# Attention's scores of layer 0 in the attention's own pair of PSUM banks

## The chip, the cores and the metric

One Trainium2 chip; the program runs on one of its cores. The metric is device time in microseconds of one execution, as the median of three runs.

## What is computed

The reference is a trunk of two layers over 256 tokens of width 2048, in float32. Each layer normalises and modulates its input, projects it, runs three mixers side by side (gated linear attention, a gated delta rule, differential attention), gates and concatenates their outputs and projects them back. Cut to what matters:

```python
for l in range(DEPTH):                                   # DEPTH = 2
    shift, scale, gate = split(c_act @ w_ada[l] + b_ada[l], 3)
    h = rms_norm(x, norm_w[l]) * (1 + scale) + shift
    (gq, gk, gv, glr, gz, dq, dk, dv, da, db, dz, aq, ak, av, az) = split(h @ w_in[l], bounds)
    o_gla = rms_norm(gla_chunked(...)) * silu(gz)        # width 512
    o_gdn = rms_norm(gated_delta_chunked(...)) * silu(dz)  # width 512
    # differential attention: 4 heads, two score maps each, D = 128, values 256 wide
    s = einsum('bhmqd,bhmkd->bhmqk', q, k) * scale       # causal
    p = softmax(s)
    o_diff = rms_norm((p[:, :, 0] - lam * p[:, :, 1]) @ v) * (1 - lam_init) * silu(az)
    y = concatenate([o_gla, o_gdn, o_diff]) @ w_out[l]
    x = x + gate * y
```

## The kernel before

The 256 tokens are two tiles of 128 (t = 0, 1). Weights come from HBM in blocks of 128x1024 (`weights`): SP issues the transfer into a ring of six raw buffers, ACT casts them to the high part `wh` (L309), DVE subtracts to get the low part `wl` (L311), and TensorE forms three products per block (high by high, high by low, low by high). The in-projection writes its results into `pt` and `pf`, the out-projection into `py`, and DVE adds `py` to the residual stream (`xr`, L1262). The out-projection runs in three phases, by the rows of w_out: phase 0 takes the linear attention's output, phase 1 the delta rule's (`ogg`), phase 2 the attention's (`odf`). Beside all this the w_ada products of the next layer run in the gaps: SP loads a block into the same ring as `rawa` (L347), DVE multiplies and sums it (L327), and ACT finishes pairs of them (`ada_j`, L339).

PSUM has eight banks in three groups: four of p for the projections, two of a and two of b (`BANKS`, handed out by `bank`). Pair a belongs to the delta rule until that has been recorded; after that `free_a()` is true and gates take it too. Pair b serves the linear attention (`o_gla`), the rope transposes, and the attention's `aT_ps` and `o_diff`. A bank is given again only when its last reader is through.

The delta rule `gdn` ends with its state update `S_ps` on TensorE, `S_gdn` on DVE (L888), `wS_ps` on TensorE, `vn` on DVE (L876), `o_gdn` on TensorE and its copy `on_gdn` on ACT (L903). Then come squares on ACT (L563), a short chain on POOL (L907 to L912) and the gate product `z` on POOL (L1036). `gate_out` transposes z into `oT_ps`, and ACT (L1046) and DVE (L1047) split it into the operands of py, of phase 1 for the delta rule (`ogg`).

The attention (`diff_attend`) has eight tiles per layer, four heads by two query tiles, two in flight at a time. A tile runs: scores into `s_ps` (TensorE), causal mask (DVE L967, ACT L969), row maximum (DVE L971, L974), two exponentials (ACT L977), the combination coefficients (DVE L980, L982) and the difference (DVE L983), transposes `aT_ps` (TensorE) copied by ACT (L989), the product with the values `o_diff` (TensorE), its copy (ACT L995) and squares (ACT L563), five small steps on POOL for `r_o` (L999 to L1003), and the scaling (DVE L1004). The last gate takes the eight tiles' output in two halves (DVE L1036, `oT_ps`, L1046, L1047, `odf`) into phase 2.

Each step is a generator that yields between pieces. A task list with urgencies records the instructions, and a scheduler with its own estimate of times then puts them in a fixed order for each engine. Every engine executes its list strictly as it is written; the waits between engines are semaphores. So a different bank for a tile can change the order in which the scheduler lists everything around it. In layer 1 the in-projection's blocks are still running while its linear attention and delta rule are on: `L654` is the copy of `o_gla` to SBUF, `L452` a copy of projected features, `L671`, `L673` and `L674` the convolution and its silu on ACT and DVE, `QK_ps` and `Z_ps` the delta rule's products.

Of the kernel before, what the change touches and what calls it, by code (L numbers as in the profile page):

```python
# [144 lines left out]
def hybrid_trunk(ctx: ExitStack, tc: tile.TileContext, x, cvec, pos, par, w_ada, w_in, w_out, w_lr, qkn, adt, cst, out):  # L145
# [23 lines left out]
    def bank(name, tag):  # L169


        return psum.tile([P, 512], F32, name=name, tag=tag, bufs=BANKS[tag])

    def tiny(name, n, bufs=2):
        return small.tile([P, n], F32, name=name, tag=name, bufs=bufs)
# [6 lines left out]
    def mm(o, lhsT, rhs, start=True, stop=True, fast=False, **kw):  # L182
        clock[0] += rhs.shape[-1] * (0.00042 if fast else 0.0017)
        return PE.matmul(o, lhsT=lhsT, rhs=rhs, start=start, stop=stop, **kw)  # L184

    def transpose(o, i):
        clock[0] += 0.11
        PE.transpose(out=o, in_=i, identity=ident)
# [82 lines left out]
    def cc(name, n=128, off=0):  # L271
        return ct[:, CST[name] + off:CST[name] + off + n]
# [102 lines left out]
    def row_power(o, v, n):  # L375
        POOL.tensor_tensor(o, v, mhalf[:, 0:n], ALU.pow)
# [170 lines left out]
    def heads(ap, n=4):  # L547
        return ap.rearrange("p (h d) -> p h d", h=n)

    def over_heads(ap, n=4, d=128):  # L550
        return ap.rearrange("p (o d) -> p o d", o=1).broadcast_to([P, n, d])
# [6 lines left out]
    def head_norm(src, n, width, r):  # L558

        for h in range(n):  # L560
            a = junk_n[0] % (256 // width) * width
            junk_n[0] += 1
            ACT.activation(junk[:, a:a + width], src[:, width * h:width * h + width], AF.Square, accum_out=r[:, h:h + 1])  # L563
# [389 lines left out]
    def diff_attend(l, o, g, on, scr, free_a):  # L953
        causal = cc("causal")
        qT = lambda t, i: o.aqk[:, t, 0, 128 * i:128 * i + 128]
        kT = lambda t, i: o.aqk[:, t, 1, 128 * i:128 * i + 128]
        yield YW[22]

        def one_tile(h, t, turn):
            W = 128 * (t + 1)  # L960
            pb = bank("s_ps", "a" if free_a() else "b")
            for m in range(2):
                for k in range(t + 1):
                    mm(pb[:, W * m + 128 * k:W * m + 128 * k + 128], qT(t, 2 * h + m), kT(k, 2 * h + m))
            s = scr[:, (1 + turn) % 7]
            sv, pv = heads(s[:, 0:2 * W], 2), heads(pb[:, 0:2 * W], 2)
            DVE.tensor_tensor(sv[:, :, W - 128:W], pv[:, :, W - 128:W], over_heads(causal, 2), ALU.add)  # L967
            if t == 1:
                ACT.copy(sv[:, :, 0:128], pv[:, :, 0:128])  # L969
            mxs = tiny("mx_s", 2)  # L970
            DVE.tensor_reduce(mxs, sv, AX.X, ALU.max)  # L971
            sc = g.sq[t][:, 2 * h:2 * h + 2]
            nb = tiny("nb", 2)
            DVE.scalar_tensor_tensor(nb, mxs, -1.0, sc, ALU.mult, ALU.mult)  # L974
            sm = tiny("sm", 2)
            for m in range(2):
                ACT.activation(sv[:, m, :], sv[:, m, :], AF.Exp, bias=nb[:, m:m + 1], scale=sc[:, m:m + 1],  # L977
                               accum_out=sm[:, m:m + 1])
            rsm = tiny("rsm", 2, 4)
            DVE.reciprocal(rsm, sm)  # L980
            cf = tiny("cf", 1)
            DVE.scalar_tensor_tensor(cf, sm[:, 0:1], nlam[:, l:l + 1], rsm[:, 1:2], ALU.mult, ALU.mult)  # L982
            DVE.scalar_tensor_tensor(sv[:, 0, :], sv[:, 1, :], cf, sv[:, 0, :], ALU.mult, ALU.add)  # L983
            yield YW[23]
            pa = bank("aT_ps", "b")
            for k in range(t + 1):
                transpose(pa[:, HS[k]], sv[:, 0, HS[k]])
            aT = scr[:, 7, 256 * (turn % 2):256 * (turn % 2) + 256]
            ACT.copy(aT[:, 0:W], pa[:, 0:W])  # L989
            yield YW[24]  # L990
            po = bank("o_diff", "b")[:, 0:256]
            for k in range(t + 1):
                mm(po, aT[:, HS[k]], o.av[:, k, 256 * h:256 * h + 256], k == 0, k == t)
            d = o.aqk[:, t, 0, 256 * h:256 * h + 256]
            ACT.copy(d, po)  # L995
            r = tiny("r_o", 1, 4)
            head_norm(d, 1, 256, r)
            rs = rsm[:, 0:1]
            POOL.tensor_tensor(r, r, rs, ALU.mult)  # L999
            POOL.tensor_tensor(r, r, rs, ALU.mult)  # L1000
            POOL.tensor_scalar(r, r, 1.0 / 256.0, EPS, ALU.mult, ALU.add)
            row_power(r, r, 1)
            POOL.tensor_tensor(r, r, rs, ALU.mult)  # L1003
            DVE.tensor_scalar(d, d, r, None, ALU.mult)  # L1004
            yield YW[25]

        running = []
        todo = [(h, t) for h in range(4) for t in range(2)]
        turn = 0
        while todo or running:  # L1010
            if todo and len(running) < 2:
                h, t = todo.pop(0)
                running.append([clock[0], one_tile(h, t, turn)])
                turn += 1
            item = min(running, key=lambda r: r[0])
            if item[0] > clock[0]:
                yield item[0] - clock[0]
                continue
            w = next(item[1], None)
            if w is None:  # L1020
                running.remove(item)
            else:
                item[0] = clock[0] + w
        for t in range(2):
            on[t] = o.aqk[:, t, 0, :]
# [64 lines left out]
    with tc.issue_after(last_fold.ins), tc.issue_after(squared.ins), tc.issue_after(spread.ins):  # L1090
# [3 lines left out]
        pb = bank("lam_ps", "a")  # L1094
# [11 lines left out]
    for l in range(L):  # L1106
# [78 lines left out]
        def free_a():  # L1185
            return run["gdn"]["done"]
# [184 lines left out]
```

## Time and profile before

| | us |
|---|---|
| median of three runs | 1107.8 (1104.52 to 1108.89) |
| profiled execution | 1106.04 |
| its span | 1103.9 |
| TensorE busy in it | 1045.9 |
| DVE busy in it | 892.6 |
| ACT busy in it | 604.2 |
| POOL busy in it | 219.5 |

The span is the time between the first and the last instruction that the profiler saw, 2.1 us less than the device time of the same execution. Starts in the rows below count from the beginning of the span. A record of TensorE is often a part of one product of the program, since a float32 product is run in several passes; a py product is one record, a score product is two.

### The profile page before, as it was taken

The numbers are of one execution on the slowest core, as the hardware profiler recorded it, in microseconds if no ns is written. First come the engines' busy times: TensorE is split into PE (matmuls) and PEld (weight loads), VectorE is DVE, ScalarE is ACT, GpSimd is POOL, SyncE is SP. The second block draws the span as 40 slices with busy tenths as digits, with TensorE's granted clock in tenths as the row PEclk, the third lists the DMA queues.
The fourth block names the chain that finished last, engine by engine and source line by source line (L and its number), as shares of the span: only waits on it lengthen the run. The fifth ranks groups of instructions, "written<-read, shape, count | busy, mean of one in ns | idle before, by whom it ended". The sixth has DMA issues, their size and how long they took to land.

```text
span 1103.9 us, 19674 instructions
## 1 busy us (share of the span) xinstructions
PE 1045.9 (95%) x7398; PEld 915.2 (83%) x7398; DVE 892.6 (81%) x1373; ACT 604.2 (55%) x1244; POOL 219.5 (20%) x279
## 2 busy tenths in 40 slices
PE   5989999999899989969898999999999999999998
PEld 5769888888898868959796777899899877889998
DVE  7899999989999878759768687676856878687974
ACT  4845544447655726446545555458554556557642
POOL 0000000040210941133430000014232244202400
PEclk9999999999999989969998999999999999999999
DMA  9989999988977646744578898796544656677462
GB/s 366 348 280 343 340 332 337 317 312 320 317 253 249 192 148 225 269 144 142 165 247 293 319 341 307 262 301 229 180 125 159 212 181 198 223 244 238 134 210 96
DMA packets 76799, 273.24 MB, mean 248 GB/s; under 512 B 8816, under 2 KB 9888, under 8 KB 76576
## 3 DMA queue, kind: packets, MB, share of 16 engines
q1 hardware_dynamic: 76416, 271.80, 71.8%
q8 instruction: 58, 0.95, 0.3%
q14 instruction: 37, 0.30, 0.1%
q10 hardware_dynamic: 288, 0.19, 0.1%
HBM read 267.76 MB, written 4.19 MB: 246 GB/s over the span
## 4 chain that ended last, share of the span: by engine, by line
PE 61%; DVE 16%; DMA 10%; issue 7%; ACT 3%; POOL 2%; DVEq 0%; ACTq 0%; POOLq 0%; SPq 0%
PE pt L184 30%; PE py L184 14%; PE pf L184 8%; DMA rawa<-in_w_ada 7%; DVE wl L311 5%; DVE rawa L327 4%; DMA raw<-in_w_in 2%; ACT wh L309 1%; PE Z_ps L184 1%; PE s_ps L184 1%; PE o_diff L184 1%; PE Y_ps L184 1%; PE o_gla L184 1%; DVE fr L327 1%; DVE on_gdn L673 1%
## 5 line engine op out<-in xcount | busy, mean ns | idle before, releaser
L309 ACT CAST wh<-raw 128x1024 fp32r<-128x1024 f32 (+2 forms) x310 | 318.0, 1028 | 283.4 <-PE pt L184 131.5
L311 DVE TENSOR_TENSOR wl<-raw,wh 128x1024 fp32r<-128x1024 f32 (+2 forms) x310 | 382.1, 1238 | 60.6 <-ACT wh L309 57.6
L184 PE MATMUL pt<-wl,hh 128*128 128x512 f32 (+1 forms) x768 | 293.0, 384 | 4.6 <-DVE wl L311 4.5
L327 DVE SCALAR_TENSOR_TENSOR rawa<-rawa,c_row 128x1024 f32<-128x1024 f32 x184 | 228.3, 1245 | 80.5 <-DMA rawa<-in_w_ada 79.4
L184 PE MATMUL pt<-wh,hl 128*128 128x512 f32 (+1 forms) x768 | 288.8, 380 | 1.2 <-DVE hl L403 1.2
L184 PE MATMUL pt<-wh,hh 128*128 128x512 f32 (+1 forms) x768 | 271.4, 383 | 8.4 <-ACT hh L401 4.3
L184 PEld LDWEIGHTS pt<-wh,hh 128*128 128x128 f32 x768 | 144.5, 190 | 40.8 <-ACT hh L401 5.3
L184 PEld LDWEIGHTS pt<-wl,hh 128*128 128x128 f32 x768 | 145.5, 190 | 39.2 <-DVE wl L311 10.6
L184 PEld LDWEIGHTS pt<-wh,hl 128*128 128x128 f32 x768 | 145.5, 190 | 30.1 <-DVE hl L403 2.0
L184 PE MATMUL pf<-hh,wl 128*128 128x256 f32 x512 | 143.8, 284 | 4.3 <-DVE wl L311 4.3
L184 PE MATMUL pf<-hh,wh 128*128 128x256 f32 x512 | 144.5, 283 | 1.5 <-ACT wh L309 1.5
L184 PE MATMUL pf<-hl,wh 128*128 128x256 f32 x512 | 145.4, 285 | 0.0
L184 PEld LDWEIGHTS pf<-hh,wl 128*128 128x128 f32 x512 | 96.2, 189 | 6.6 <-DVE wl L311 5.3
L184 PE MATMUL py<-ogg,wh 128*128 128x256 f32 x512 | 98.4, 288 | 0.8 <-DVE z L454 0.8
L184 PEld LDWEIGHTS pf<-hh,wh 128*128 128x128 f32 x512 | 97.1, 190 | 2.5 <-ACT wh L309 1.7
L184 PEld LDWEIGHTS pf<-hl,wh 128*128 128x128 f32 x512 | 96.9, 189 | 2.1 <-issue 1.3
L184 PE MATMUL py<-odf,wh 128*128 128x256 f32 x512 | 88.6, 278 | 2.0 <-ACT odf L1046 1.7
L184 PEld LDWEIGHTS py<-ogg,wh 128*128 128x128 f32 x512 | 80.3, 189 | 2.2 <-DVE z L454 1.2
L184 PEld LDWEIGHTS py<-odf,wh 128*128 128x128 f32 x512 | 77.3, 188 | 2.9 <-ACT odf L1046 2.1
L339 ACT ACTIVATE ada_j<-ada_p,pt 128x2 f32<-128x2 f32 x96 | 31.3, 326 | 79.2 <-DVE rawa L327 75.3
L184 PE MATMUL py<-ogg,wl 128*128 128x256 f32 x256 | 72.0, 283 | 0.0
L184 PE MATMUL py<-odf,wl 128*128 128x256 f32 x256 | 70.6, 277 | 0.0
(277 smaller groups left out, 1340.9 us busy)
## 6 DMA issues: line engine op xcount, KB each, us to landing
raw<-in_w_in SPq DMA_DIRECT2D x224, 512.0 KB, 4.9
rawa<-in_w_ada SPq DMA_DIRECT2D x184, 512.0 KB, 4.7
raw<-in_w_out SPq DMA_DIRECT2D x64, 512.0 KB, 4.4
raw<-in_w_in SPq DMA_DIRECT2D x20, 402.0 KB, 4.4
fr<-in_w_ada SPq DMA_DIRECT2D x8, 512.0 KB, 9.2
xt<-in_x SPq DMA_DIRECT2D x4, 512.0 KB, 5.8
xr<-in_x SPq DMA_DIRECT2D x4, 512.0 KB, 7.0
xs<-xr SPq DMA_DIRECT2D x1, 2048.0 KB, 7.2
```

What stands on the lines that cost most here:

```text
L184: return PE.matmul(o, lhsT=lhsT, rhs=rhs, start=start, stop=stop, **kw)
L309: ACT.copy(wh, raw)
L311: DVE.tensor_tensor(wl, raw, wh.bitcast(F32), ALU.subtract)
L327: DVE.scalar_tensor_tensor(raw, raw, 1.0, cb, ALU.mult, ALU.mult, accum_out=sums[:, i:i + 1])
L339: ACT.activation(tiny("ada_j", 2), sums[:, 2 * f:2 * f + 2], AF.Identity, bias=bias, scale=scale, accum_out=o)
L673: DVE.scalar_tensor_tensor(yi[:, s:T], src[:, 0:T - s], pcol("conv", w + 3 - s), yi[:, s:T], ALU.mult, ALU.add)
```

## The change

In layer 0 the score tiles `s_ps` always take a bank of pair b. In layer 1 they do as before: pair a, once the delta rule has been recorded.

```diff
@@ -958,7 +958,7 @@
 
         def one_tile(h, t, turn):
             W = 128 * (t + 1)
-            pb = bank("s_ps", "a" if free_a() else "b")
+            pb = bank("s_ps", "a" if l > 0 and free_a() else "b")
             for m in range(2):
                 for k in range(t + 1):
                     mm(pb[:, W * m + 128 * k:W * m + 128 * k + 128], qT(t, 2 * h + m), kT(k, 2 * h + m))
```

In layer 0 the eight score tiles, which all took pair a, take pair b. The number of instructions is the same on every engine. The order in which the scheduler lists them differs on TensorE, DVE, ACT and POOL; on SP it is the same. The names in the rows carry the program's buffer numbers.

TensorE, at the end of the delta rule of layer 0, before:

```order
L184 MATMUL py_4947<-ogg_4126,wl_4895 128x256
L184 MATMUL S_ps_4636<-vn_4384,kn_3080 128x128 x4
L184 MATMUL wS_ps_4703<-S_gdn_4641,wT_4398 64x128 x4
L184 MATMUL o_gdn_4760<-vn_4384,E_2875 64x128 x8
L184 MATMUL o_gdn_4760<-S_gdn_4479,fm_187 64x128
```

and with the change:

```order
L184 MATMUL S_ps_4636<-vn_4384,kn_3080 128x128 x4
L188 MATMUL aT_ps_4989<-ct_83,scr_2099 128x128 x2
L184 MATMUL o_diff_5165<-av_190,scr_2099 128x256
L184 MATMUL o_diff_5176<-av_190,scr_2099 128x256 x2
L184 MATMUL s_ps_5188<-aqk_189 128x128 x2
L184 MATMUL s_ps_5218<-aqk_189 128x128 x4
L184 MATMUL wS_ps_4703<-S_gdn_4641,wT_4398 64x128 x4
L184 MATMUL o_gdn_4760<-vn_4384,E_2875 64x128 x8
```

The transposes, value products and scores of the attention's first tiles (5188 and 5218 are the scores of the third and fourth) now stand between the delta rule's last state update and the product that waits for it.

ACT around the copy of the delta rule's output (L903) in layer 0, before:

```order
L309 CAST wh_5070<-raw_5068 128x1024
L339 ACTIVATE ada_j_5338,ada1_140<-ada_p_5027,pt_81 128x2
L903 COPY on_gdn_4780<-o_gdn_4760 128x512
L563 ACTIVATE junk_113,ss_gdn_4782<-on_gdn_4780 128x128 x4
L339 ACTIVATE ada_j_5340,ada1_140<-ada_p_5027,pt_81 128x2
L969 COPY scr_2099<-s_ps_4928 128x2x128
```

and with the change:

```order
L339 ACTIVATE ada_j_5338,ada1_140<-ada_p_5027,pt_81 128x2
L977 ACTIVATE scr_2099,sm_5196<-scr_2099,nb_5194,sc_d_3615 128x128
L977 ACTIVATE scr_2099,sm_5229<-scr_2099,nb_5227,sc_d_3628 128x256 x2
L977 ACTIVATE scr_2099,sm_5196<-scr_2099,nb_5194,sc_d_3615 128x128
L903 COPY on_gdn_4780<-o_gdn_4760 128x512
L563 ACTIVATE junk_113,ss_gdn_4782<-on_gdn_4780 128x128 x4
L339 ACTIVATE ada_j_5340,ada1_140<-ada_p_5027,pt_81 128x2
L563 ACTIVATE junk_113,r_o_5168<-aqk_189 128x256
L563 ACTIVATE junk_113,r_o_5180<-aqk_189 128x256
```

Exponentials of the third and fourth tiles stand ahead of L903, and squares of the first two tiles' outputs (`r_o`) come right behind the delta rule's squares, after an L339.

ACT in layer 1, where the linear attention's outputs (`o_gla`) are copied from pair b, before:

```order
L309 CAST wh_8257<-raw_8255 128x1024
L654 COPY scr_7121<-o_gla_8949 128x2x128
L563 ACTIVATE junk_113,ss_gla_8958<-scr_7121 128x128 x2
L654 COPY scr_7121<-o_gla_8986 128x2x128
L452 COPY fm_6165<-pf_8090 128x256
L563 ACTIVATE junk_113,ss_gla_9041<-scr_7121 128x128
L671 ACTIVATE on_gdn_8317<-fm_6165,pt_81 128x256
L563 ACTIVATE junk_113,ss_gla_9041<-scr_7121 128x128
L654 COPY scr_7121<-o_gla_9030 128x2x128
```

and with the change:

```order
L309 CAST wh_8257<-raw_8255 128x1024
L452 COPY fm_6165<-pf_8090 128x256
L671 ACTIVATE on_gdn_8317<-fm_6165,pt_81 128x256
L674 ACT_TABLE_LOAD
L674 ACTIVATE fm_6165<-on_gdn_8317 128x512
L339 ACTIVATE ada_j_8757,ada1_140<-ada_p_7989,pt_81 128x2
L654 COPY scr_7121<-o_gla_8949 128x2x128
```

The convolution's steps with a table load, and an L339 that belongs to a w_ada product, now stand ahead of the copy of o_gla_8949. On TensorE `QK_ps` (behind L674) now stands ahead of the third product in question, o_gla_9030.

## Rows read from the trace of the kernel before

**Rows 1.** The page, section 1: busy us (share of the span) xinstructions
```profile
PE 1045.9 (95%) x7398; PEld 915.2 (83%) x7398; DVE 892.6 (81%) x1373; ACT 604.2 (55%) x1244; POOL 219.5 (20%) x279
```

**Rows 2.** Busy us (xinstructions) per engine in stretches, then PE clock, DMA share, GB/s
```profile
470.00:480.00 10.00, 6.64 (x51) 5.22 (x51) 7.16 (x14) 1.44 (x3) 3.67 (x3) 0.73 0.80 248
...
480.00:490.00 10.00, 3.83 (x24) 2.73 (x22) 5.15 (x10) 4.48 (x16) 5.13 (x7) 0.67 0.38 123
...
500.00:520.00 20.00, 20.00 (x169) 19.75 (x168) 19.33 (x49) 14.86 (x39) 7.18 (x10) 1.00 0.45 141
...
526.00:540.00 14.00, 10.45 (x76) 9.06 (x75) 9.01 (x18) 5.66 (x17) 7.38 (x19) 1.00 0.46 150
...
820.00:1100.00 280.00, 280.00 (x2090) 250.12 (x2089) 206.88 (x315) 152.59 (x321) 66.00 (x88) 1.00 0.59 191
```

**Rows 3.** Timeline of TensorE: start, us, line, op, out<-in [idle before <-releaser]
```profile
477.19 1.96 PE L184 MATMUL o_gdn<-vn,E 64*64 64x128 f32 x14 [2.01 <-DVE vn L876]
...
487.07 0.45 PE L188 MATMUL oT_ps<-ct,z 128*128 128x128 f32 x1 [4.17 <-DVE scr L967]
...
496.33 0.36 PE L184 MATMUL py<-ogg,wh 128*128 128x256 f32 x1
...
497.82 1.05 PE L184 MATMUL s_ps<-aqk 128*128 128x128 f32 x8
```

**Rows 4.** Timeline of DVE, same stretch
```profile
473.03 1.11 DVE L888 SCALAR_TENSOR_TENSOR S_gdn<-S_gdn,cd,S_ps 128x128 f32<-128x128 f32 x4
...
474.06 1.21 DVE L311 TENSOR_TENSOR wl<-raw,wh 128x1024 fp32r<-128x1024 f32 x1
...
485.23 1.23 DVE L327 SCALAR_TENSOR_TENSOR rawa<-rawa,c_row 128x1024 f32<-128x1024 f32 x1 [4.25 <-DMA rawa<-in_w_ada]
...
486.50 0.42 DVE L967 TENSOR_TENSOR scr<-s_ps,ct 128x256 f32<-128x256 f32 x1
```

**Rows 5.** Timeline of ACT and POOL, same stretch
```profile
481.11 0.58 ACT L903 COPY on_gdn<-o_gdn 128x512 f32<-128x512 f32 x1 [4.26 <-PE o_gdn L184]
...
487.43 1.26 POOL L1036 TENSOR_TENSOR z<-z,on_gdn 128x512 f32<-128x512 f32 x1
```

**Rows 6.** Timeline of ACT and TensorE at layer 0's end
```profile
530.62 0.37 ACT L995 COPY aqk<-o_diff 128x256 f32<-128x256 f32 x1 [0.82 <-PE o_diff L184]
...
535.79 0.87 PE L188 MATMUL oT_ps<-ct,z 128*128 128x128 f32 x6 [1.10 <-DVE z L1036]
...
538.12 0.38 PE L184 MATMUL py<-odf,wh 128*128 128x256 f32 x1 [0.16 <-DVE odf L1047]
```

**Rows 7.** Timeline of TensorE, ACT, SP and DVE in layer 1
```profile
813.04 0.66 PE L184 MATMUL o_gla<-scr,fm 64*64 64x128 f32 x8
...
815.26 0.60 PE L184 MATMUL o_gla<-mix,scr 128*128 128x128 f32 x4
...
817.32 1.28 ACT L674 ACT_TABLE_LOAD   x1
...
815.36 0.33 SPq L347 DMA_DIRECT2D rawa<-in_w_ada  x1
...
818.86 1.23 DVE L327 SCALAR_TENSOR_TENSOR rawa<-rawa,c_row 128x1024 f32<-128x1024 f32 x1 [1.26 <-DMA rawa<-in_w_ada]
```

**Rows 8.** Line L673 (ns min/median/max, first and last start), and the rawa transfer
```profile
L673 DVE SCALAR_TENSOR_TENSOR on_gdn<-fm,pt,on_gdn x72: 458/477/1372, 258.2 to 865.5; 128x255 f32<-128x255 f32 x24, 128x254 f32<-128x254 f32 x24, 128x253 f32<-128x253 f32 x24
...
DMA to landing us min/median/max: 3.4/4.7/10.2
```

**Rows 9.** Stretches as in rows 2: after idle time, early in the program
```profile
280.00:283.70 3.70, 1.88 (x15) 1.68 (x14) 3.70 (x6) 1.44 (x3) 0.00 (x0) 0.97 0.85 313
...
283.70:287.00 3.30, 3.30 (x18) 3.30 (x17) 3.30 (x6) 0.00 (x0) 0.00 (x0) 0.51 0.96 287
...
391.70:396.00 4.30, 0.18 (x4) 0.21 (x4) 2.56 (x6) 0.13 (x1) 1.70 (x2) 1.00 0.01 5
...
396.30:406.20 9.90, 9.87 (x46) 7.19 (x47) 9.30 (x15) 2.23 (x4) 2.34 (x3) 0.50 0.55 168
```

## The prediction

> **What bounds the kernel now.** I read the totals first, then a table by stage, then single stretches of the engines' timelines. The totals [rows 1] say that TensorE is busy for 95% of the span, so only its idle time and its slow clock can be won back or added to. The table by stage [rows 2] says where those are. In layer 0, between 470 and 490 us, TensorE is busy for 6.64 and 3.83 of 10 us each at a granted clock of 0.73 and 0.67; between 526 and 540 it misses another 3.6 us. In layer 1, from 820 to 1100, it is busy all the time at full clock: a stall put into layer 1 has nothing behind it that could take it up, and it goes whole to the end.
>
> The idle time of 470 to 490 is the end of the delta rule [rows 3]: o_gdn waits 2.01 us for vn, and the gate's transposes start at 487.07 after 4.17 us of waiting. The DVE timeline [rows 4] says why: L888 ends at 474.14, and the first L967, the attention's first work on its scores, comes only at 486.50, behind a w_ada product that waited 4.25 us for its DMA. ACT takes o_gdn at 481.11 and POOL's gate product z ends at 488.69 [rows 5]. Unbroken py begins at 496.33 [rows 3]. The last attention tile of the layer then sets a second end: its copy L995 starts at 530.62 and py resumes at 538.12, 7.5 us later [rows 6].
>
> **What the change does.** Eight score tiles of layer 0 take their banks from the pair b, which aT_ps and o_diff use as well. No instruction is added or taken away. The scores no longer wait in the recorded order for the delta rule's pair, so the scheduler lists the attention's first six tiles earlier, and it lists one place of layer 1 otherwise too, where no line changed.
>
> **Layer 0, up to the restart of py.** The first pair of tiles costs DVE 0.42 us for L967, about as much for its second, and with the later steps about 3.85 us (an estimate from the lengths of the same steps between 486.5 and 492.6). This now stands in DVE's queue before 476, where DVE is nearly full, and one wl product of 1.21 us [rows 4] has moved ahead of L888. Bounds of the delay of S_gdn are 1.2 us (the rest goes into gaps) and 5.1 us (nothing does); following the order with the durations of before I get 3.1. The score, aT and o_diff matmuls that now stand between S_ps and wS_ps lie inside that wait and cost nothing; if S_gdn came 3 us sooner they would be late by up to 2.9 us. vn and o_gdn follow 2.6 us later. ACT's copy of o_gdn (L903) now stands behind four exponentials of the next tiles, so it comes at 484.4 instead of 481.1 [rows 5]. POOL's chain from there to z has small r_o operations put between its steps, and these wait for ACT squares queued behind an L339 that waits for a w_ada product on DVE. I put the end of z at 495.7 (495 to 497), not 488.7. From the first oT_ps behind the last gate product to py the tail of before needs 2.3 us [rows 6]; I take 2.7 for a slower clock, so py runs from 498.4, 2.1 us later than before.
>
> **Up to phase 1's end.** Behind the restart stand the same 188 py matmuls (counted in the order) at 0.118 us (20 us for 169, [rows 2]), 22.2 us. But of the attention only 3.95 us of PE work is left there, since the scores of the first six tiles and four o_diff are already done; before it was 6.6. Both are counts from the order, at 0.22 us for a score product (eight records, four products, in 0.81 us from start to start, [rows 3]), twice that for an o_diff, and 0.11 for a transpose. 498.4 + 22.2 + 3.95 is 524.6; before, 496.3 + 22.2 + 6.6 is 525.1. That is a gain of 0.5 us.
>
> **The tail of layer 0.** Before, 33 of 36 py matmuls of the first odf half (3.9 us) stand behind the last o_diff and cover part of its chain of 7.5 us; now they stand ahead of it. The last o_diff ends at 530.1 to 531.2 (530.6 before), its chain is the same, and py resumes at 537.6 to 538.4: the chain sets the end both times. Layer 0 therefore comes out at zero, with bounds of -1.5 and +2.5 from the bounds of z. The idle time of TensorE there is no longer cut into pieces of about 1 us but lies in one piece of 4 to 5 us. Two places show what an idle stretch does. After 1.88 busy of 3.70 us the clock was 0.51 for 3.3 us, which costs 1.65; after 4.1 idle us it was 0.50 for 9.9, which costs 5 [rows 9]. The tail of before kept its clock with 3.6 idle us in pieces (a clock of 1.00 from 526 to 540, [rows 2]). Bounds are 0 and 5; I take 0.8, half the price of the nearer, shorter row.
>
> **Layer 1.** At about 810 ACT's order has changed. The copy L654 that frees the b bank for the third o_gla of this place now stands behind L452, L671, a table load, L674 and an L339. Before, that copy came ahead of all these, and the third o_gla ran at 815.26 with TensorE never idle [rows 7]. Now L674 needs the three L673 steps on DVE (0.48 each, [rows 8]), which follow a wl and end at about 813.8. With the table load of 1.28 us [rows 7] and L674, the QK matmuls that PE has next start at about 815.7, while PE is through with the second o_gla at 813.7 [rows 7]: 2.0 us idle. L339 needs a w_ada product whose transfer is issued after that wl, at 811.95. The same transfer took 3.5 us before (issue 815.36, product 818.86) [rows 7]; with it the product ends at 816.7, L339 at 817.1, L654 at 817.5, and the third o_gla starts then instead of after 0.7 us of QK and pf: 1.1 us more. The sum is 3.1 us. Its bounds come from the transfer: the shortest of the trace is 3.4 us and the longest 10.2 [rows 8], which would give 9.8; the median, 4.7, would give 4.3. I keep 3.5, since DMA is nearly idle there. It would fall to 2.0 if L339 were not late. For the clock after two idle pieces of 2 and 1 us I take 0.8 again (0 to 1.65, [rows 9]). In layer 1 nothing is behind it that waits [rows 2].
>
> **The sum.** 0 (layer 0) + 0.8 (clock, tail) + 3.1 (layer 1) + 0.8 (clock) is 4.7 us. The profiled execution took 1106.0 us, so 1110.7 against it; the median of the three runs is 1107.8, 1.8 above, and the forecast against it is 1112.5.
>
> The Trainium skill (Perfetto Trace Analysis, Matmul Optimizations) says "Ensure all 8 PSUM banks are being leveraged to maximize available instruction-level parallelism"; by this rule the change should cost, as three users share two banks in layer 0 while the other pair is free. The idle time of 480 to 490 has a DVE instruction behind it and not a bank [rows 3], so I give the rule no term of its own in layer 0; in layer 1 its kind of wait, for a b bank, is the term of 3.1.
>
> **Rivals.** (1) Layer 0 is a gain that stays. The attention's work fills the idle time of the delta rule; POOL's chain is not disturbed, z ends 2.6 us later and not 7, at 491.3, and py starts at 494.0, 4.4 us ahead of my restart; phase 1 ends 4.9 us before that of before. It needs POOL and ACT to run r_o's operations in gaps and the last tiles to keep up, and the stall of layer 1 to be hidden by an earlier transfer: 1107.8 - 4.9 gives 1103. For it: the 9.5 idle us of 470 to 490 [rows 2]. Against it: the order itself, in which z stands behind r_o steps that need later ACT work, and a tail that is bound by the last tile. The Trainium skill (Perfetto Trace Analysis, Optimization Strategy) says of kernels with several regimes that performance may be improved by interleaving them; it speaks for this rival, and the order shows interleaving, but also what was put in the way of the delta rule.
>
> (2) Nothing that can be measured: the transfer in layer 1 is issued sooner than I think, the QK matmuls wait under 1 us, and layer 0 is at zero: 1107 to 1109.
>
> (3) Slower by much. The mechanism is the clock at the end of layer 0: its idle time in one piece is followed by 10 us at half clock as at 396 to 406 [rows 9], 5 us; with layer 1's 3.1 and its clock at 1.65 that is 9.8, so 1117.6. It decides once the piece comes near the 4.1 us of that row.
>
> (4) The change does not do what it says: the order lists another place for nearly every score, so this has no chance worth a number over 0.01.
>
> **How the numbers follow.** The forecast has 0.47, and lies between +1.5 and +7.5 us. About 0.5% (5.5 us) is what a measurement of this kernel can tell from no change; of the forecast 0.27 lies within it and 0.20 above. Rival 1 has 0.14 (faster), rival 2 has 0.18 (same), rival 3 has 0.20 (slower), rival 4 has 0.01 (same). That makes faster 0.14, same 0.46, slower 0.40. The range from 1102.5 to 1118 leaves out about half of rivals 1 and 3, near 0.17.
>
> **What would show it.** In the changed kernel's trace: S_gdn (L888) ending near 477 and z (L1036 of the gdn gate's second half) ending near 496; unbroken py from about 498; a single idle piece of over 4 us on TensorE before the last oT_ps of layer 0, with py after it at about 538 and the clock in the next 10 us; in layer 1, some 10 us after the stage's Z_ps, an idle piece before QK_ps and one before o_gla, released by ACT. Wrong would be: z under 492, no idle time in layer 1, or a time under 1104.

## The result: 0.6% slower

The changed kernel takes 1114.4 us (median of five executions; 1111.65 to 1115.12), against 1107.8 before (five executions as well). The ratio is 1.0061, with a 95% interval of 1.0039 to 1.0084, so about 6.7 us more. It was timed a second time beside the experiments and gave 1.0074 (1.0058 to 1.0091). The ratios leave out the few executions that took far longer than the others of the same kernel. The forecast was 1112.5, with 4.7 us more. The profiled execution has a span of 1112.5 us, 8.6 above the span before.

The totals of the page after the change (busy us, share of the span, instructions) answer to [rows 1]:

```profile
PE 1052.9 (95%) x7398; PEld 920.1 (83%) x7398; DVE 893.0 (80%) x1373; ACT 605.5 (54%) x1244; POOL 210.2 (19%) x279
```

TensorE is busy for 7.0 us more with the same number of instructions, while DVE and ACT stay within 1.3. The mean granted clock of the whole span is 0.982 both times, so a lower mean clock is not the reason; it counts whether the clock is low where TensorE works or where it waits. The table by stage (busy us and instructions per engine, then granted clock, DMA share, GB/s) shows where, beside [rows 2]:

```profile
470.00:480.00 10.00, 9.26 (x66) 7.77 (x64) 9.89 (x18) 4.23 (x9) 5.87 (x5) 1.00 0.85 240
480.00:490.00 10.00, 3.71 (x35) 2.48 (x35) 5.63 (x17) 5.62 (x26) 1.63 (x5) 0.75 0.40 134
...
526.00:540.00 14.00, 7.43 (x43) 5.76 (x42) 7.40 (x13) 3.57 (x11) 3.52 (x10) 0.86 0.48 151
540.00:550.00 10.00, 9.84 (x70) 9.49 (x69) 6.56 (x9) 4.68 (x7) 1.84 (x2) 0.85 0.22 57
812.00:818.00 6.00, 4.32 (x84) 3.59 (x82) 3.09 (x6) 3.66 (x6) 0.00 (x0) 1.00 0.30 87
818.00:826.00 8.00, 7.47 (x65) 6.77 (x66) 1.31 (x3) 4.28 (x18) 4.69 (x7) 0.59 0.22 68
```

The last three stretches in the kernel before:

```profile
540.00:550.00 10.00, 9.84 (x85) 9.56 (x84) 9.12 (x12) 6.64 (x10) 2.98 (x3) 1.00 0.50 154
812.00:818.00 6.00, 6.00 (x54) 5.25 (x54) 3.42 (x4) 4.30 (x16) 3.32 (x3) 1.00 0.23 79
818.00:826.00 8.00, 8.00 (x118) 7.56 (x116) 4.83 (x7) 5.13 (x11) 4.10 (x4) 1.00 0.46 142
```

From 470 to 480 TensorE is filled now (9.26 us instead of 6.64), from 480 to 490 it is as idle as before, and from 526 to 540 it is busy for 3.0 us less, at a lower clock. In layer 1, where it was never idle from 812 to 826, it now lacks 1.68 us and 0.53 us and runs for most of the second stretch at half clock.

**The front of layer 0.** The timeline of TensorE at the end of the delta rule, beside [rows 3]:

```profile
473.19 1.16 PE L184 MATMUL S_ps<-vn,kn 64*128 64x128 f32 x8
...
480.88 1.08 PE L184 MATMUL o_gdn<-vn,E 64*64 64x128 f32 x14 [1.58 <-DVE vn L876]
...
486.79 0.47 PE L188 MATMUL oT_ps<-ct,z 128*128 128x128 f32 x1 [3.54 <-ACT on_gdn L903]
...
498.41 0.39 PE L184 MATMUL py<-ogg,wh 128*128 128x256 f32 x1 [0.52 <-DVE ogg L1047]
```

Here DVE, ACT and POOL of the same stretch, which answer to [rows 4, 5]:

```profile
477.19 1.11 DVE L888 SCALAR_TENSOR_TENSOR S_gdn<-S_gdn,cd,S_ps 128x128 f32<-128x128 f32 x4
...
482.70 1.23 DVE L327 SCALAR_TENSOR_TENSOR rawa<-rawa,c_row 128x1024 f32<-128x1024 f32 x1 [0.82 <-DMA rawa<-in_w_ada]
...
484.04 0.49 ACT L977 ACTIVATE scr<-scr,nb,sc_d 128x128 f32<-128x128 f32 x1 [3.51 <-DVE nb L974]
...
486.18 0.56 ACT L903 COPY on_gdn<-o_gdn 128x512 f32<-128x512 f32 x1
...
493.75 1.27 POOL L1036 TENSOR_TENSOR z<-z,on_gdn 128x512 f32<-128x512 f32 x1
```

S_gdn starts 4.2 us later than before. L903, the copy of the delta rule's output, comes at 486.18 instead of 481.11. The last product of o_gdn had ended at 483.0, but the copy stands behind four exponentials, and these wait for `nb`, which DVE forms only behind a w_ada product that waited for its transfer. The gate product z ends at 495.0 and unbroken py starts at 498.4. Starts like these differ by some us between traces of one order, as the experiments show below.

**The tail of layer 0.** DVE, ACT and TensorE, beside [rows 6]:

```profile
531.87 1.23 DVE L327 SCALAR_TENSOR_TENSOR rawa<-rawa,c_row 128x1024 f32<-128x1024 f32 x1 [2.34 <-DMA rawa<-in_w_ada]
...
533.14 0.39 ACT L339 ACTIVATE ada_j<-ada_p,pt 128x2 f32<-128x2 f32 x1 [2.61 <-DVE rawa L327]
...
533.52 0.35 ACT L995 COPY aqk<-o_diff 128x256 f32<-128x256 f32 x1
...
530.86 1.02 PE L184 MATMUL o_diff<-av,scr 128*128 128x256 f32 x4
534.31 0.44 PE L188 MATMUL oT_ps<-ct,z 128*128 128x128 f32 x2 [2.43 <-DVE z L1036]
537.36 1.54 PE L188 MATMUL oT_ps<-ct,z 128*128 128x128 f32 x6 [2.61 <-DVE z L1036]
539.47 1.37 PE L184 MATMUL py<-odf,wh 128*128 128x256 f32 x4 [0.56 <-ACT odf L1046]
540.63 0.42 PE L184 MATMUL py<-odf,wl 128*128 128x256 f32 x1
```

The last o_diff ran from 530.86 to 531.88. Its copy L995 could follow then, but an L339 stands ahead of it, which waits for a w_ada product whose transfer came late: L995 runs at 533.52, 1.6 us after its data. TensorE waits in two pieces of 2.4 and 2.6 us and resumes py at 539.47. That is the first of four products; [rows 6] shows the fourth of before, at 538.12, and these are its first and the last o_diff of before:

```profile
529.45 1.13 PE L184 MATMUL o_diff<-av,scr 128*128 128x256 f32 x4 [0.63 <-ACT scr L989]
...
537.33 0.62 PE L184 MATMUL py<-odf,wh 128*128 128x256 f32 x3 [0.67 <-ACT odf L1046]
```

Like for like, py resumes 2.1 us later than before. From the end of the last o_diff to it there are 7.6 us, before 6.75: of the 1.6 us lost at the copy, 0.8 arrive. In the fence of the changed kernel, the length 0.42 of a single py, 0.28 at full clock, shows the half clock behind that.

**Layer 1.** SP, DVE and TensorE at the place that the change did not touch, beside [rows 7]:

```profile
814.26 0.33 SPq L347 DMA_DIRECT2D rawa<-in_w_ada  x1
...
817.74 1.23 DVE L327 SCALAR_TENSOR_TENSOR rawa<-rawa,c_row 128x1024 f32<-128x1024 f32 x1 [1.87 <-DMA rawa<-in_w_ada]
...
818.89 0.41 DVE L812 TENSOR_TENSOR Tm<-Tm,Z_ps 128x256 f32<-128x256 f32 x1
...
817.92 0.45 PE L184 MATMUL QK_ps<-fm 128*64 128x64 f32 x8 [1.69 <-ACT fm L674]
...
819.45 0.44 PE L184 MATMUL Y_ps<-Um,C 64*64 64x64 f32 x2 [0.53 <-DVE Tm L812]
819.82 1.22 PE L184 MATMUL o_gla<-mix,scr 128*128 128x128 f32 x4
```

QK_ps waits 1.69 us for L674. Then Y_ps waits 0.53 us for `Tm` (L812), which stands on DVE behind the late w_ada product. From 819.8 to 826.2 TensorE is never idle but runs at half clock: four o_gla take 1.22 us, where they took 0.60 [rows 7].

### The profile page after: what moved, and what is told of

Read it like the earlier page. It is cut to its first block, busy times and chain, and to the rows that moved or that the text cites. A ratio compares the mean times of both kernels' runs of the same rounds, so it can differ in the third digit from the quotient of the medians.

```text
span 1112.5 us, 19679 instructions
## 1 busy us (share of the span) xinstructions
PE 1052.9 (95%) x7398; PEld 920.1 (83%) x7398; DVE 893.0 (80%) x1373; ACT 605.5 (54%) x1244; POOL 210.2 (19%) x279
## 5 line engine op out<-in xcount | busy, mean ns | idle before, releaser
L327 DVE SCALAR_TENSOR_TENSOR rawa<-rawa,c_row 128x1024 f32<-128x1024 f32 x184 | 229.5, 1252 | 76.0 <-DMA rawa<-in_w_ada 75.7
L184 PE MATMUL py<-odf,wh 128*128 128x256 f32 x512 | 90.9, 281 | 0.7 <-ACT odf L1046 0.6
L339 ACT ACTIVATE ada_j<-ada_p,pt 128x2 f32<-128x2 f32 x96 | 31.2, 325 | 77.9 <-DVE rawa L327 74.2
```

Source lines behind the costliest of these rows:

```text
L327: DVE.scalar_tensor_tensor(raw, raw, 1.0, cb, ALU.mult, ALU.mult, accum_out=sums[:, i:i + 1])
L339: ACT.activation(tiny("ada_j", 2), sums[:, 2 * f:2 * f + 2], AF.Identity, bias=bias, scale=scale, accum_out=o)
```

## The experiments

The order of each engine can be held fixed by a table of instructions at the end of the program. It adds no wait, only an order in which the scheduler lists them. With it one layer could be given the order of one kernel and the other layer that of the other. Diffs of an order show only the instructions that change places. All ratios are to the kernel before, timed on the same chip; one per cent is 11 us.

### The two layers apart

The first kernel (e1) is the changed one with the order of before in layer 1. The second (e2) is the kernel before, with its banks, and the changed kernel's order in layer 1 alone.

> The changed kernel, but with layer 1's instructions held in the order of before on every engine; layer 0 stands as in the changed kernel. Theory A (two separate places, layer 0 worth about 4.5 us by the two profiles, layer 1 about 4.2): 1108 + 2.5 to 4.5, so 1110 to 1112, a stall-free stretch from 810 to 830. Rival B (all of it is layer 1; layer 0's difference between the profiles is what two runs differ by): 1107 to 1109. Rival C (all of it is layer 0): 1114.

Measured: 1.0013 (0.9998 to 1.0028), +1.4 us (-0.2 to +3.1). Theory A, with 2.5 us or more for layer 0, misses; rival B fits.

> The kernel before, bank choice included, but with layer 1's instructions held in the order that the changed kernel has there. Theory A: 1108 + 4.2, so 1112, with idle time ahead of QK_ps and of Y_ps near 815 to 820 and a low clock behind. Rival B: 1114. Rival C: 1108.

Measured: 1.0050 (1.0031 to 1.0069), +5.5 us (3.4 to 7.6). The two waits of layer 1 are there, as in the changed kernel:

```profile
816.61 0.45 PE L184 MATMUL QK_ps<-fm 128*64 128x64 f32 x8 [1.68 <-ACT fm L674]
818.18 0.44 PE L184 MATMUL Y_ps<-Um,C 64*64 64x64 f32 x2 [0.58 <-DVE Tm L812]
```

The sum of the two is 6.9 us. The whole, timed again (e11):

> The changed kernel itself beside e9 and e10 on the same chip, so that parts and whole stand on one scale: 1113 to 1115. The parts e1 (+1.4 us) and e2 (+5.5 us) add up to 6.9, so 1.006 of the kernel before.

Measured: 1.0074 (1.0058 to 1.0091), +8.2 us (6.4 to 10.1); its own trace has the same wait of QK_ps, 1.69 us, but Y_ps does not wait in it. So the loss lies in layer 1 for the greater part, and there it needs no bank: the second kernel has every bank as before.

### What the loss of layer 1 consists of

Three more kernels keep the kernel before in layer 0, start from the changed order in layer 1 and move a few instructions. The first (e5) lets TensorE do the third o_gla before QK_ps:

```diff
-QK_ps, first Y_ps
 pf x3
 o_gla_9030
+QK_ps, first Y_ps
```

> The kernel of e2 (layer 0 of before, layer 1 in the changed kernel's order) with one more exchange on TensorE: QK_ps and the first Y_ps behind the third o_gla. Theory A (two engines' queues hold TensorE up at this place: ACT by L674 and by L339, and taking one wait away only meets the next): the wait for L674 goes, but the third o_gla then waits for its copy behind L339, so some 3 us are idle in one piece and the clock falls as in e2: 1112, within 1.5 us. Rival (the wait for L674, 1.7 us, is the cause): 1108 to 1109.

Measured: 1.0044 (1.0027 to 1.0060). The wait for L674 has gone, and one for L654, longer than both others together, is in its place:

```profile
815.61 1.22 PE L184 MATMUL o_gla<-mix,scr 128*128 128x128 f32 x4 [2.97 <-ACT scr L654]
```

The second (e6) takes the w_ada product out of the way: on ACT L339 goes behind the copies of o_gla, on DVE L327 behind L812.

```diff
-L339 ACTIVATE ada_j<-ada_p,pt
 L654 COPY scr<-o_gla
+L339 ACTIVATE ada_j<-ada_p,pt
-L327 SCALAR_TENSOR_TENSOR rawa<-rawa,c_row
 L812 TENSOR_TENSOR Tm<-Tm,Z_ps
+L327 SCALAR_TENSOR_TENSOR rawa<-rawa,c_row
```

> The kernel of e2 with the w_ada product and its L339 put behind the work they stand in front of: L339 behind the copies of o_gla on ACT, the product L327 behind the update of Tm (L812) on DVE. TensorE's order as in e2. Theory A: the second idle piece (0.6 us) goes and the first (1.7 us, L674) stays. If the clock falls on the first piece alone, 0.6 us come back: 1111.5. If it takes both, the clock stays up and about 4 us come back: 1108. Rival (the w_ada product is the whole cause): 1107, no idle time at all.

Measured: 1.0031 (1.0014 to 1.0047), which overlaps the interval without this edit. Only the wait for L674 is left:

```profile
814.79 0.45 PE L184 MATMUL QK_ps<-fm 128*64 128x64 f32 x8 [1.69 <-ACT fm L674]
```

The third (e7) makes both edits and also puts the copy L654 of o_gla_8949 ahead of L674 with its table load.

> e5 and e6 together, and the copy of the second o_gla ahead of L674 on ACT; the rest of layer 1 stays in the changed kernel's order. Theory A: the two waits at this place are all that layer 1's new order costs: 1107 to 1108.5, no idle piece over 0.5 us between 805 and 830, clock at 1.00 there. Rival (something else in the new order of layer 1 costs as well, later on): 1110 or more.

Measured: 0.9985 (0.9968 to 1.0001). TensorE is not idle there. The stretches 812 to 818 and 818 to 826 show idle time and clock together (columns as in the table by stage above). First the changed order of layer 1, unedited:

```profile
812.00:818.00 6.00, 3.92 (x49) 2.93 (x43) 4.05 (x8) 2.65 (x5) 0.00 (x0) 1.00 0.28 87
818.00:826.00 8.00, 7.82 (x64) 7.39 (x65) 0.04 (x1) 4.01 (x18) 5.68 (x7) 0.57 0.21 68
```

QK_ps later:

```profile
812.00:818.00 6.00, 3.03 (x21) 2.25 (x21) 1.57 (x3) 4.30 (x15) 1.33 (x3) 0.80 0.45 152
818.00:826.00 8.00, 8.00 (x101) 7.57 (x100) 1.01 (x1) 2.73 (x7) 4.36 (x5) 0.72 0.01 2
```

L339 and L327 later:

```profile
812.00:818.00 6.00, 4.32 (x50) 3.56 (x51) 2.27 (x5) 4.35 (x14) 1.88 (x3) 0.90 0.44 131
818.00:826.00 8.00, 8.00 (x97) 7.68 (x94) 1.55 (x2) 2.67 (x9) 3.82 (x5) 0.86 0.14 38
```

Both, and L654 earlier:

```profile
812.00:818.00 6.00, 5.89 (x80) 4.93 (x80) 2.98 (x7) 4.74 (x17) 1.57 (x3) 1.00 0.32 97
818.00:826.00 8.00, 8.00 (x113) 7.60 (x112) 3.37 (x4) 3.90 (x9) 5.28 (x5) 1.00 0.38 128
```

The idle time is each stretch less its busy time. The clock's cost is each stretch times what its clock lacks to 1, for instance 8 x 0.43 = 3.4 in the unedited order. For the four and for the changed kernel:

| order of layer 1 | idle, us | lost by clock, us | sum | timed against before, us |
|---|---|---|---|---|
| changed kernel (both layers) | 2.2 | 3.3 | 5.5 | +6.7 and +8.2, with layer 0 |
| unedited, layer 0 as before | 2.3 | 3.4 | 5.7 | +5.5 (3.4 to 7.6) |
| QK_ps later | 3.0 | 3.4 | 6.4 | +4.9 (3.0 to 6.6) |
| L339, L327 later | 1.7 | 1.7 | 3.4 | +3.4 (1.5 to 5.2) |
| both, L654 earlier | 0.1 | 0.0 | 0.1 | -1.7 (-3.5 to +0.1) |

The sums agree with the times within their intervals, and the clock costs as much as the waits or more. With the idle time the half clock goes too, so here it followed the idle time and not something else of the new order.

How much it costs is not fixed by the wait. Three more traces have the changed order of layer 1: the second timing of the changed kernel (e11) and the two kernels of the next section that start from it (e3, e4). In all three the wait for L674 is the only one, 1.68 or 1.69 us as with L339 and L327 later. Yet the clock takes 3.4 us in e11 and e4 and 5.1 in e3, not 1.7. This is e11:

```profile
812.00:818.00 6.00, 4.31 (x67) 3.48 (x63) 3.85 (x6) 2.95 (x5) 0.00 (x0) 0.96 0.28 87
818.00:826.00 8.00, 7.95 (x67) 7.22 (x67) 0.55 (x3) 4.28 (x18) 5.44 (x7) 0.61 0.24 68
```

So the 1.7 of that row of the table is one trace, and what moving L339 and L327 alone is worth stays open.

The Trainium skill (Perfetto Trace Analysis, Matmul Optimizations) says that power is scaled with use and that it is "important that matmuls execute back-to-back in batches"; the last row of the table agrees: 0.1 us idle, a clock of 1.00.

### What bounds layer 0

First the L339 that stands ahead of the last copy of layer 0, in the changed kernel (e3):

```diff
+L995 COPY aqk<-o_diff_5504
 L339 ACTIVATE ada_j_6062<-ada_p
-L995 COPY aqk<-o_diff_5504
```

> The changed kernel with two neighbours exchanged on ACT at the end of layer 0: the copy of the last o_diff (L995) ahead of the L339 that waits for a w_ada product. All else as in the changed kernel. Theory A: the copy waited about 1.6 us behind L339 (533.52 instead of 531.9), so py resumes 1.6 us sooner, the idle piece is shorter and the clock may stay up: 1111.5 to 1113. Rival (the last tile is late for another reason, and something else is late next): 1114.

Measured: 1.0057 (1.0040 to 1.0074), 0.4 us below the changed kernel and 1.9 below its second timing, neither of which these intervals can tell from nothing. The trace shows the chain shortened, on ACT and TensorE:

```profile
530.92 0.37 ACT L995 COPY aqk<-o_diff 128x256 f32<-128x256 f32 x1 [1.39 <-PE o_diff L184]
...
537.77 1.37 PE L184 MATMUL py<-odf,wh 128*128 128x256 f32 x4 [0.56 <-ACT odf L1046]
```

From the end of the last o_diff, 530.88, to py there are 6.9 us here, against 7.6 in the changed kernel. So 0.7 us are won at this place and not the 1.6 of theory A; the waits for z remain, and the timing cannot show so little.

Then the front (e4). The changed kernel, layer 1 included, with the delta rule's last links first: on DVE L888 ahead of a wl product and vn ahead of the next tiles' L967, on ACT L903 with its squares ahead of the exponentials, on POOL the chain to z ahead of the steps of r_o, on TensorE wS_ps ahead of the scores.

```diff
+L903 COPY on_gdn, L563 ACTIVATE junk x4
 L339 ACTIVATE ada_j_5338
 L977 ACTIVATE scr x4
-L903 COPY on_gdn, L563 ACTIVATE junk x4
```

> The changed kernel, scores of layer 0 in pair b as there, with the delta rule's last links put ahead of the attention's work on each engine: S_gdn ahead of the wl product, vn ahead of the masks, the copy of o_gdn and its squares ahead of the next tiles' exponentials, the gate product on POOL ahead of r_o. Layer 1 is held as in the changed kernel. Theory A (the order put in the delta rule's way costs, not the bank): z ends at 489 to 490 instead of 495, py runs from about 493 instead of 498.4, and 2 to 5 us come back: 1109 to 1112. Rival D (the two banks shared by three users cost, or the last tile's chain sets the end whatever the front does): 1114, with idle time at the end of the layer grown by what the front won.

Measured: 1.0090 (1.0070 to 1.0110). POOL and TensorE of this run:

```profile
485.54 1.26 POOL L1036 TENSOR_TENSOR z<-z,on_gdn 128x512 f32<-128x512 f32 x1
...
491.98 0.56 PE L184 MATMUL py<-ogg,wh 128*128 128x256 f32 x1
...
529.53 0.45 PE L188 MATMUL aT_ps<-ct,scr 128*128 128x128 f32 x1 [4.30 <-DVE scr L983]
...
539.64 1.37 PE L184 MATMUL py<-odf,wh 128*128 128x256 f32 x4 [0.56 <-ACT odf L1046]
```

py restarts at 491.98, 6.4 us earlier than in the changed kernel's profile (5.4 counted from the last S_ps in each trace, see below), and nothing of it arrives; theory A misses. A w_ada product (from 525.49, after its transfer), its L339 and the last tile's exponentials (from 527.15) stand one behind the other, TensorE waits 4.3 us for the tile's `scr`, and py resumes at 539.6 as before the edit, after a stretch at low clock: 0.55 from 526 to 540. The last tile sets the end, and the front's gain is only waited away there.

Two kernels with layer 1 in the order of before put the attention steps of the last two tiles ahead of the weight products and L339 around them. One does so alone (e9), and one with the edit of the front too (e10).

> The kernel of e1 (layer 0 of the changed kernel, layer 1 of before) with the last two attention tiles of layer 0 put first: their maxima, coefficients and differences on DVE ahead of neighbouring wl and w_ada products, the last exponentials and the last copy of o_diff on ACT ahead of L339, the last w_ada product of the stage behind the last gate product. Theory A (the last tile's chain sets the end of layer 0): the last copy L995 starts 3 to 5 us sooner against the restart of py, the idle time before the last oT_ps shrinks, the clock may stay up there: 1102 to 1105. Rival (weights or the clock set that end): 1107 to 1108 as e1.

Measured: 0.9993 (0.9976 to 1.0010).

> e4's front (the delta rule's last links first) and e9's tail together, layer 1 held in the order of before. Theory A: what e4 won at the front (py from 492 instead of 498) now reaches the end of the layer, since the last tile no longer holds it: 1100 to 1104, faster than both kernels. Rival (another limit stands behind the last tile, such as DVE's wl products or the transfers): 1106 to 1108, with idle time that those release.

Measured: 0.9990 (0.9976 to 1.0004), not the 1104 or less of theory A. TensorE of this last run:

```profile
494.24 0.56 PE L184 MATMUL py<-ogg,wh 128*128 128x256 f32 x1
...
535.31 0.96 PE L188 MATMUL oT_ps<-ct,z 128*128 128x128 f32 x6 [1.90 <-DVE z L1036]
536.85 1.37 PE L184 MATMUL py<-odf,wh 128*128 128x256 f32 x4 [0.58 <-ACT odf L1046]
```

Neither kernel can be told from before. Starts on the clock of the profile do not tell what these edits did, since a whole trace is early or late by some us: the first kernel of all (e1), with the changed kernel's layer 0 and neither edit, resumes py at 535.88, a microsecond ahead of this one. Counted from the start of the last S_ps of layer 0 in each trace:

| layer 0 | runs | to unbroken py of phase 1, us | to the first py at the tail, us |
|---|---|---|---|
| as before | before, e2, e5, e6, e7 | 24.8 to 26.1 | 65.7 to 67.4 |
| as changed | changed, e1, e11 | 24.3 to 25.2 | 65.6 to 66.3 |
| L995 ahead of L339 | e3 | 24.6 | 64.6 |
| front edit | e4 | 19.9 | 67.5 |
| tail edit | e9 | 24.8 | 62.0 |
| both | e10, and e12 below | 19.4 to 19.8 | 62.5 to 62.9 |

The front edit wins 5 us at the front and none at the tail, with the tail edit or without it. The tail edit shortens this stretch by 3 to 4 us, but the times do not confirm it: 0.9993 (e9) against 1.0013 (e1), with overlapping intervals. What holds the tail once the last tile comes early stays open; TensorE still waits 1.90 us for z there.

### The banks themselves

In layer 0 the first four score tiles take pair b, the last four pair a again (e8). Layer 1 has the order of before.

```diff
-            pb = bank("s_ps", "a" if l > 0 and free_a() else "b")
+            pb = bank("s_ps", "a" if (l > 0 or turn >= 4) and free_a() else "b")
```

> The bank choice changed once more: in layer 0 the first four score tiles take pair b, the last four pair a as in the kernel before; layer 1 is held in the order of before. Theory A (layer 0's end is set by the last tile's chain, whatever the front does; banks matter only by the order that the scheduler makes of them): within 0.3% of the kernel before unless its last tile is listed earlier, 1104 to 1109. Rival D (two banks for three users hold the last tiles up): the last tiles come earlier with their own pair and 3 us or more are won against e1, 1103 to 1104.

Measured: 0.9993 (0.9975 to 1.0011), against 1.0013 with all eight in pair b (e1). Those intervals overlap. Its front is as late as in the changed kernel (six oT_ps at 495.98 after waiting 1.89 us for z), so giving the later tiles their old banks back does not bring py forward. The new banks with the order of before in layer 0, or the reverse, were not tried.

The trace of the changed kernel shows what TensorE waits for. In layer 0 only one of its waits, 0.2 us, can be for a reader that empties a bank of pair b (scores behind L995). The long bank waits are in pair a, before and after. The transposes oT_ps take their banks there and read only z. In the kernel before they wait 4.17 us for L967 [rows 3], which reads the scores out of pair a; in the changed kernel 3.54 us for L903, which reads o_gdn out of it. So three users of pair b hardly hold TensorE up there, in the order that the scheduler made for them. What that order costs against another with the same banks stays open.

### All repairs together

The last kernel (e12) has the new banks, the two edits of layer 0 and the edited order of layer 1.

> The changed kernel with every repair of the study at once: in layer 0 the delta rule's last links first and the attention steps of the last two tiles first, and in layer 1 the new order with the QK products, L339, L327 and L654 moved. The repairs of layer 0 alone gave 0.999 of the kernel before and those of layer 1 alone 0.9985. If the two are independent their differences of -1.1 and -1.6 us add up to -2.7, a ratio near 0.9975, and the trace shows no idle time in layer 1 between 805 and 832. If what they save is only the clock of the particular order in each run, the ratio stays at 0.998 to 1.000. In both cases TensorE is idle before the last oT_ps of layer 0, about 2 us before each z, as the last tile's chain still sets the end there.

Measured: 1.0001 (0.9981 to 1.0020). No idle time appears in layer 1 from 795 to 835, so the repairs hold there, but the -1.1 and -1.7 us of the parts do not add up to a gain. The best supported reading is that each is zero. No version here beats the kernel before.

## Why the prediction was right

The side came out right: +6.7 us timed, +4.7 forecast with +1.5 to +7.5 around it. The second timing, +8.2 (6.4 to 10.1), lies a little above that. The size is near because errors in layer 1 cancelled in part, which is luck. The parts stand as follows.

**Up to the restart of py: right, and closer than it deserves.** Unbroken py from 498.4 was forecast, and it came at 498.41; z was to end at 495.7 and ended at 495.0. On the way two steps were put too early: S_gdn was to end near 477 and ended at 478.3, and L903 was put at 484.4 and came at 486.18. The four exponentials ahead of it were counted, but not that they wait for a w_ada product on DVE. POOL's chain then took less than the estimate, so that the errors nearly cancelled. The hit to a tenth is luck as well: in the four other traces with this front (e1, e3, e9, e11) unbroken py starts between 494.9 and 498.8, in the five with the front of before between 494.2 and 497.8. The means are 1.1 us apart, where 2.1 were forecast. In e1, z ends at 491.4, which the prediction would have taken as a sign of being wrong.

**Up to phase 1's end: right.** 524.6 was forecast; phase 1's last py starts at 524.40 (520.9 to 524.8 in those four traces). One price was off on the way: four score products in 0.81 us are 0.20 each, not 0.22.

**The tail: one queue missed.** The last o_diff ends at 531.9, forecast 530.1 to 531.2. "Its chain is the same" was wrong: an L339 now stands ahead of L995 and holds it up by 1.6 us, of which 0.8 reach py. It resumes at 539.5, where the forecast of 537.6 to 538.4 even meant the fourth product. The idle time of 4 to 5 us that was forecast in one piece came in two, 2.4 and 2.6. The clock term was 0.8 (0 to 5). By this trace it is nearer 2: the six oT_ps take 0.67 us more than in [rows 6], and the 2.5 us of py from 540.6 to 543.1 are at half clock, 1.2 lost. Layer 0 as a whole was forecast at 0 + 0.8 and timed at +1.4 (-0.2 to +3.1), which neither confirms the difference nor excludes zero. Counted from S_ps to the tail it is as long as before, 65.6 to 66.3 us against 65.7 to 67.4, which fits the zero, though what stands ahead of S_ps differs between the orders.

**Layer 1, the waits: place right, size too large.** The wait for L674 was put at 2.0 us and is 1.69. The transfer took 3.5 us as assumed (issue 814.26, product 817.74). The second wait was put at 1.1 us, for L654 behind L339. What stood first on TensorE was a Y_ps that waits for L812, behind the same w_ada product on DVE, 0.53 us; by then the third o_gla had nothing left to wait for. That makes 2.2 us instead of 3.1, and in three of the four other traces of this order (e3, e4, e11) the second wait is missing, which makes 1.7. The late w_ada product is behind the second wait wherever there is one.

**Layer 1, the clock: the term that was mis-sized.** It was 0.8, with a bound of 1.65 from the nearest row [rows 9], and it measured 3.3 to 3.4 in the traces of the changed kernel, e2 and e4, and 5.1 in that of e3. The row chosen had 1.8 idle us spread over 3.7, and the time at half clock behind it was 3.3 us. Here 2.2 idle us in two pieces were followed by 6.4 us at half clock, and 1.7 in one piece by about as much (e11). The other row, with 4.1 idle us and 9.9 at half clock behind it, should have been the upper bound in this place too, as it was for the tail. The sum was near because the waits were put too high and the clock too low; of 3.9 for layer 1, 5.5 were measured.

**The rivals.** The first, a gain of layer 0 that stays, put py at 494.0 and fell at its restart at 498.4; one trace of the same front comes near (494.9, e1), but its layer 0 is no faster. The run that won 5 us at the front shows why: the last tile takes the gain away. With the tail edit added the time was 0.9990 (0.9976 to 1.0004), so no gain is shown that way either. The Trainium skill's advice to interleave stages (Perfetto Trace Analysis, Optimization Strategy) spoke for it; interleaving did fill the idle time of 470 to 480, but not the chain that ends the layer. The second failed in layer 1, where QK_ps waited 1.69 us and not under 1. The third, 10 us of half clock at the tail, did not come in the first profile: the half clock there ended at 543, 5.7 us after the six oT_ps began, and some of those us were idle. In the second trace of the same kernel (e11) it did:

```profile
526.00:540.00 14.00, 7.75 (x43) 6.22 (x44) 7.33 (x13) 3.57 (x11) 3.58 (x10) 0.79 0.48 150
540.00:550.00 10.00, 9.82 (x65) 9.56 (x65) 5.63 (x7) 4.51 (x7) 2.13 (x2) 0.78 0.19 58
```

By the same arithmetic these are 5.1 us, as the rival had it, part of them in idle time. Its total of 9.8 us was still above both timings, and its price of the clock in layer 1, 1.65, was too low. The Trainium skill's rule on the eight PSUM banks (Perfetto Trace Analysis, Matmul Optimizations) was rightly given no term of its own, since 5.5 of the loss came with the old banks, but the reason given was wrong: the wait of 4.17 us in [rows 3] is one for a bank of pair a, which L967 empties. It cost little, since z ended only at 488.69 and the six transposes behind it need z.

## What to carry over

Where a scheduler lists the whole program, a change of one resource can move work in stages that it does not touch; compare the order of every stage, since here most of the loss was in the other layer. A wait put into a stage in which TensorE is always busy cost here its own length and from one to three times as much again in clock, so price both, with every row that shows the clock after a wait. Ahead of each urgent copy or product, look on its engine for work that hangs on a transfer: L339 and L327 stood there in three of the four places that lost time. Compare stages by distances within one trace, not by their starts.

## What was not expected

- One idle piece of 1.69 us on TensorE, busy before it, had no fixed price. Half clock (1.2 GHz instead of 2.4) followed it for about 3.4 us with L339 and L327 later, 6.7 in e11 and 10.2 in e3, which is 1.7 to 5.1 us lost. In the tail of the kernel before, 3.55 idle us within 14, in pieces of about 1 us, left the clock at 1.00 [rows 2]; with the same order of layer 0 in e2, 2.5 idle us there went with 0.88.
- Single stages of one profile scatter more than the whole. Four experiments have layer 0 exactly as before, and their TensorE is busy from 480 to 490 for 4.09 to 6.02 us, where the profile of before shows 3.83. Part of that is a shift of the whole program by a microsecond or two against the slices. Gains and losses of a stage below 2 us were therefore taken from the timed ratios.
